# RWKV-7 mixer of a two-layer trunk: block inverse kept on VectorE, R and V projections moved among the first two chunks, VectorE and ScalarE in written order

## The chip, the cores and the metric

One NeuronCore of a Trainium2 chip. Its engines each run their own instruction stream: TensorE (PE, matmuls; PEld, its weight loads), VectorE (DVE), ScalarE (ACT), GpSimd (POOL) and SyncE (SP, which here only issues DMAs; ACT and POOL issue some too). The metric is the device time of one execution in microseconds; the times given are medians of three runs.

## The reference

The reference is a decoder trunk of two layers on 256 tokens of 1024 features. Each layer is LN(alpha x + SwiGLU/2), LN(alpha x + mixer), LN(alpha x + SwiGLU/2). The mixer of layer 0 is a spatial gating MLP, that of layer 1 is RWKV-7, which is where the change lies:

```python
r, k, v = jnp.einsum('nbsd,nde->nbse', x_rkv, w_rkv)      # six token-shift mixes of x
w = -jax.nn.softplus(-(w0 + jnp.tanh(xw @ w1) @ w2)) - 0.5
a = jax.nn.sigmoid(a0 + (xa @ a1) @ a2)
g = jax.nn.sigmoid(xg @ g1) @ g2
kk = normalise(k * k_k);  k = k * (1 + (a - 1) * k_a)
decay = jnp.exp(-jnp.exp(w))
# per head (16 heads x 64), token by token:
state = state * decay + (state @ -kk) (kk * a)^T + v k^T;   y = state @ r
y = group_norm(y) ; bonus = sum(r * k * r_k) * v
out = ((y + bonus) * g) @ w_o
```

## The kernel before

The recurrence is computed in four chunks of 64 tokens (two to each token tile `m` of 128). Within a chunk the token-by-token dependence is a unit-triangular system of 64x64 per head. Its matrix, the products of ZR (columns of -kk and r, decayed) with KBT (k and kk a, divided by the decay), is masked (`ab`) and cut into blocks of 32x32; the inverse of the 128 diagonal blocks is found on VectorE by 31 steps of two operations (`i0` to `i30`, L1034 and L1036), with one block in each partition; `H` holds the inverses. Getting from the masked matrix (tokens in partitions) to that layout (block in partition) goes through DRAM: `ab` writes to `dA` (GpSimd's queue), `iload` reads `M` (ScalarE's queue); afterwards `iout` writes `dH` and `dG` and reads `G` and `Hf` (SyncE's queue). `od0`, `od1`, `oe0`, `oe1` then compute the off-diagonal blocks on PE from `G`, `Hf` and the masked matrix. Each chunk `c` then runs `av` and `x` (right-hand side X), `u` (X times the inverse `Hf`, into VU), `s` (the state for the next chunk) and `y` (the output); `on` normalises the output per head on VectorE with a power operation on GpSimd in the middle (`rs`), `ga` makes the gate, `og` multiplies, `oc` transposes for the output projection `O`.

Projections run in units of 128 input rows x 1024 weights, one DMA of 512 KB each. K and the output projection multiply hi/lo pairs (three matmuls, L221 to L223); for them a weight unit is rounded by ScalarE (`wh`, L118) and its rest taken by VectorE (`wl`, L119). R and V run in plain float32 (L301) from the loaded unit itself.

Two things set the order. PE and SyncE run in program order, which the hand-written string ORDER gives: each word is an operation, `R011` is R, half 0, token tile 1, part 1. ACT, VectorE and GpSimd are ordered by a scheduler from dependencies. Weight loads and roundings are put in by `Stream.advance` some units ahead of their use (`ahead`). PSUM banks are two `tp`, two `mm` and four `acc`.

```python
        DX, DW, DA, DI, DO = A, nc.sync, G, A, nc.sync     # queues of decay_x, decay_w, ab, iload, iout
```

## Time and profile before

| | us |
|---|---|
| median of 3 runs (1144.19 to 1144.59) | 1144.59 |
| the profiled execution's own time | 1143.73 |
| its span, first to last instruction | 1142.0 |
| PE busy | 1103.9 |
| VectorE busy | 698.7 |
| ScalarE busy | 480.5 |
| GpSimd busy | 42.2 |

The RWKV mixer's own instructions lie between about 727 and 947 us of the span. Busy time of PE counts a matmul from its start to its modelled end, and the granted clock says in which of its two speeds PE ran (1.00 is 2.4 GHz, 0.50 is 1.2 GHz).

### The profile page before, as it was taken

What the parts mean: (1) busy time and instruction counts of PE and PEld (TensorE: products, weight loads), DVE (VectorE), ACT (ScalarE), POOL (GpSimd) and SP (SyncE); (2) the same over time, 40 slices, a digit from 0 to 9 for tenths busy, and PEclk for the clock granted to TensorE, in tenths of its full rate; (3) what the DMA queues carried; (4) which work ended last, traced back from release to release, by engine and by line L of the source; (5) the groups of instructions that cost most, each with busy time, mean ns of one, the idle gap of its engine ahead of it and who ended that gap; (6) DMA issues with size and microseconds to landing.
All of it is one profiled execution on the core that took longest, in us unless ns stands there. A gap on an engine that the chain in (4) does not pass through costs nothing.

```text
span 1142.0 us, 15347 instructions
## 1 busy us (share of the span) xinstructions
PE 1103.9 (97%) x5860; PEld 879.1 (77%) x5860; DVE 698.7 (61%) x969; ACT 480.5 (42%) x636; POOL 42.2 (4%) x44
## 2 busy tenths in 40 slices
PE   8999999999999999999999999999989889999997
PEld 5888888778888788888888888775555668788885
DVE  6654556769658555457655453878655787555544
ACT  5544443455335444444444452462123245444430
POOL 0000000100000000000000000112100110000000
PEclk9999999999999999999999999999999989999999
DMA  8776565775645766655677563437876146766530
GB/s 289 236 235 185 185 197 168 232 268 196 208 148 155 240 206 198 186 183 157 197 221 225 183 202 124 166 93 256 271 203 237 43 129 191 239 204 196 184 111 38
DMA packets 153933, 216.51 MB, mean 190 GB/s; under 512 B 21213, under 2 KB 114845, under 8 KB 153858
## 3 DMA queue, kind: packets, MB, share of 16 engines
...
q0 software_dynamic: 1024, 3.15, 1.0%
...
HBM read 209.46 MB, written 3.42 MB: 186 GB/s over the span
## 4 chain that ended last, share of the span: by engine, by line
PE 81%; DVE 7%; DMA 5%; issue 2%; ACT 2%; POOL 1%; ACTq 0%; SPq 0%; DVEq 0%; POOLq 0%
PE mm L221 15%; PE mm L223 15%; PE mm L222 15%; PE acc L221 8%; PE acc L222 8%; PE acc L223 8%; PE mm L301 3%; DMA raw<-ffn_w_in 2%; DVE wl L119 2%; PE tp L415 2%; POOL rs L259 1%; PE tp L235 1%; ACT wh L118 1%; DMA raw<-rwkv_w_rkv 1%; PE tp L577 1%
## 5 line engine op out<-in xcount | busy, mean ns | idle before, releaser
L119 DVE TENSOR_TENSOR wl<-raw,wh 128x1024 fp32r<-128x1024 f32 (+1 forms) x332 | 396.2, 1209 | 267.1 <-ACT wh L118 259.8
L118 ACT CAST wh<-raw 128x1024 fp32r<-128x1024 f32 (+1 forms) x332 | 340.3, 1041 | 340.8 <-PE acc L223 146.0
L221 PE MATMUL mm<-wh,xh 128*128 128x512 f32 x832 | 327.3, 393 | 5.5 <-ACT wh L118 2.4
L222 PE MATMUL mm<-wl,xh 128*128 128x512 f32 x832 | 324.7, 390 | 0.6 <-DVE wl L119 0.6
L223 PE MATMUL mm<-wh,xl 128*128 128x512 f32 x832 | 325.1, 391 | 0.2 <-DVE xl L228 0.2
L221 PEld LDWEIGHTS mm<-wh,xh 128*128 128x128 f32 x832 | 156.5, 188 | 41.5 <-ACT wh L118 3.9
L223 PEld LDWEIGHTS mm<-wh,xl 128*128 128x128 f32 x832 | 156.6, 188 | 34.6 <-DVE xl L228 1.9
L222 PEld LDWEIGHTS mm<-wl,xh 128*128 128x128 f32 x832 | 156.7, 188 | 33.1 <-DVE wl L119 1.3
L221 PE MATMUL acc<-wh,hT 128*128 128x512 f32 x352 | 141.4, 402 | 0.0
L222 PE MATMUL acc<-wl,hT 128*128 128x512 f32 x352 | 137.4, 390 | 0.0
L223 PE MATMUL acc<-wh,hT 128*128 128x512 f32 x352 | 137.4, 390 | 0.0
L404 ACT ACTIVATE h<-mm 128x256 f32<-128x256 f32 x88 | 33.8, 384 | 106.0 <-PE mm L223 105.9
L223 PEld LDWEIGHTS acc<-wh,hT 128*128 128x128 f32 x352 | 66.1, 188 | 14.8
L222 PEld LDWEIGHTS acc<-wl,hT 128*128 128x128 f32 x352 | 66.2, 188 | 12.6
L221 PEld LDWEIGHTS acc<-wh,hT 128*128 128x128 f32 x352 | 66.1, 188 | 12.7
L405 DVE TENSOR_TENSOR h<-h,mm 128x256 f32<-128x256 f32 x88 | 36.8, 418 | 59.8 <-ACT h L404 59.8
L301 PE MATMUL mm<-raw,mix 128*128 128x512 f32 x128 | 59.4, 609 | 0.9 <-DMA raw<-rwkv_w_rkv 0.9
L259 POOL TENSOR_TENSOR rs<-ve,mhalf 128x1 f32<-128x1 f32 x14 | 14.2, 1011 | 926.2 <-DVE ve L267 926.2
L301 PEld LDWEIGHTS mm<-raw,mix 128*128 128x128 f32 x128 | 23.6, 193 | 26.6 <-issue 23.8
L228 DVE TENSOR_TENSOR hT<-tp,hT 128x512 fp32r<-128x512 f32 x44 | 30.2, 686 | 7.6 <-ACT hT L227 7.6
L227 ACT CAST hT<-tp 128x512 fp32r<-128x512 f32 x44 | 25.9, 588 | 9.0 <-PE tp L415 8.9
L227 ACT CAST xh<-tp 128x512 fp32r<-128x512 f32 x24 | 13.2, 588 | 34.9 <-PE tp L235 34.9
...
## 6 DMA issues: line engine op xcount, KB each, us to landing
...
```

Source lines behind the costliest of these rows:

```text
L118: i = nc.scalar.copy(h[:, s], raw[:, s])
L119: j = nc.vector.tensor_tensor(l[:, s], raw[:, s], h[:, s].bitcast(F32), op=ALU.subtract)
L221: i = mm(out, lhsT=lh, rhs=rh, start=start, stop=False)
L222: mm(out, lhsT=lh, rhs=rl, start=False, stop=False)
L223: mm(out, lhsT=ll, rhs=rh, start=False, stop=stop)
L227: i = self.nc.scalar.copy(h, src)
L228: return i, self.nc.vector.tensor_tensor(l, src, h.bitcast(F32), op=ALU.subtract)
L259: self.nc.gpsimd.tensor_tensor(rs, v, self.mhalf[:, :w], op=ALU.pow)
L301: i = self.nc.tensor.matmul(ps, lhsT=xs[:, c], rhs=h[:, s], start=kk == 0, stop=kk == 7)
L404: nc.scalar.activation(hb[:, o + 256:o + 512], ps[:, 0:256], AF.Silu)
L405: nc.vector.tensor_tensor(hb[:, o:o + 256], hb[:, o + 256:o + 512], ps[:, 256:512], op=ALU.mult)
L415: nc.tensor.transpose(ps[:, o:o + P], st["h"][c][:, hh:hh + P], self.ident)
```

## The change

From `iload` to `free` VectorE and ScalarE keep the order in which the program is written, by dependencies that need no semaphore (class `Ordered`; its wrapper is at L149, so the changed kernel's instructions of the mixer carry that line); weight roundings are included. `ab` writes two tensors, `Aof` (off-diagonal blocks) and `D` (diagonal blocks, part of which ScalarE copies into place), and `M`, `G` and `Hd` are made by VectorE's 32x32 transposes; all DRAM copies of the inverse are gone. `Hf` is cleared by GpSimd instead of VectorE, and filled by two VectorE and two GpSimd copies for each token tile (`hf0`, `hf1`). R's PSUM is copied out by ScalarE (`rk`), its two products follow as `rm` and `rb`. `on` is cut in two, `on` up to the root and `oz` for the multiply with it. The `Ex` DMAs of `decay_x` go from ScalarE's queue to SyncE's. `od`, `oe` and `u`, `s` of the first two chunks use `acc` banks. R and V parts are single units, and those not done before the inverse is out are placed among the chunks; `x` comes ahead of `av`. `a:N` in ORDER sets how far roundings run ahead.

```diff
-                i = nc.scalar.copy(h[:, s], raw[:, s])
-                j = nc.vector.tensor_tensor(l[:, s], raw[:, s], h[:, s].bitcast(F32), op=ALU.subtract)
+                i = self.A.copy(h[:, s], raw[:, s])
+                j = self.V.tensor_tensor(l[:, s], raw[:, s], h[:, s].bitcast(F32), op=ALU.subtract)
...
+class Ordered:
+    def __init__(self, b, eng):
+        self.b, self.eng, self.on, self.last = b, eng, False, None
+    def __getattr__(self, name):
+        fn = getattr(self.eng, name)
+        def f(*args, **kw):
+            i = fn(*args, **kw)
+            if self.on:
+                if self.last is not None:
+                    self.b.after(i, self.last)
+                self.last = i
+            return i
+        return f
...
+        V, A = self.ws.V, self.ws.A = Ordered(self, nc.vector), Ordered(self, nc.scalar)
...
-                R, bo = st["R"][m]
-                rk = self.s4("rk")[:, 0:512]
-                s = slice(h * 512, h * 512 + 512)
-                V.tensor_tensor(R[:, s], ps, st["E"][m][0][:, s], op=ALU.mult)
-                V.tensor_tensor(rk, ps, st["kp"][m][:, s], op=ALU.mult)
+                    st["rk", m] = self.s4("rk")
+                s = half(h)
+                A.copy(st["rk", m][:, s], ps)
+            return f
+        def rmul(m, h):
+            def f():
+                R, s = st["R"][m][0], half(h)
+                (V.tensor_tensor(R[:, s], st["rk", m][:, s], R[:, s], op=ALU.mult))
+            return f
+        def rbonus(m, h):
+            def f():
+                s = half(h)
+                rk, bo = st["rk", m][:, s], st["R"][m][1]
+                (V.tensor_tensor(rk, rk, st["kp"][m][:, s], op=ALU.mult))
...
+                if c == 0 and m == 0:
+                    st["D"], st["Aof"] = self.s4("D"), self.s4("Aof")
+                b0 = (m * 16 + c * 8) * 32
+                D, Of = (st[k][:, b0:b0 + 256] for k in ("D", "Aof"))
...
-                masked(t[:, half(c)], ps, self.mask[:, 0:64])
-                if c == 0:
-                    return
-                t3 = t.rearrange("p (b z) -> p b z", z=64)
-                for blk in range(2):
-                    for e in range(2):
-                        b0 = blk * 64 + e * 32 + m * 16
-                        r0 = e * 64 + blk * 32
-                        DA.dma_start(self.dA[b0:b0 + 16].rearrange("b s t -> s b t"),
-                                    t3[r0:r0 + 32, :, blk * 32:blk * 32 + 32])
+                p3 = ps.rearrange("p (b t) -> p b t", b=8)
+                for out, k in ((Of, 32), (D, 0)):
+                    V.tensor_tensor(out.rearrange("p (b t) -> p b t", b=8), p3[:, :, k:k + 32],
+                                    self.mask[:, k:k + 32].unsqueeze(1).broadcast_to([P, 8, 32]), op=ALU.mult)
+                for e in range(2):
+                    r = slice(e * 64 + 32, e * 64 + 64)
+                    A.copy(D[r, :], Of[r, :])
...
-            DI.dma_start(st["M"], self.dA.rearrange("b s t -> b (s t)"))
+            V.on = A.on = True
+            V.transpose(st["M"].rearrange("p (s t) -> p t s", s=32), st["D"].rearrange("p (b t) -> p t b", b=32))
...
-                V.memset(t, 0.0)
+                G.memset(t, 0.0)
...
-            Mt, Ht = st["M"], st["H"]
-            M3, H3 = (t.rearrange("p (s t) -> p s t", s=32) for t in (Mt, Ht))
-            q = DO
-            q.dma_start(self.dH.rearrange("b s t -> b (s t)"), Ht)
-            V.tensor_copy(M3[0:64], H3[0:64].rearrange("p s t -> p t s"))
-            Hf = st["Hf"]
-            q.dma_start(self.dG.rearrange("b s t -> b (s t)"), Mt[0:64, :])
-            Gt = self.s4("G")
-            st["G"] = Gt
-            def back(m, blk, e):
-                b0 = blk * 64 + e * 32 + m * 16
-                r0 = e * 64 + blk * 32
-                q.dma_start(
-                    Hf[m].rearrange("p (b t) -> p b t", t=64)[r0:r0 + 32, :, blk * 32:blk * 32 + 32],
-                    self.dH[b0:b0 + 16].rearrange("b s t -> s b t"))
-            for e in range(2):
-                q.dma_start(Gt.rearrange("p (b t) -> p b t", t=32)[e * 64:e * 64 + 32],
-                            self.dG[e * 32:e * 32 + 32].rearrange("b s t -> s b t"))
-            for m in range(2):
-                for blk in range(2):
+            H = st["H"]
+            t = self.s4("G")
+            (V.transpose(t.rearrange("p (b s) -> p s b", b=32), H.rearrange("p (s t) -> p s t", s=32)))
+            st["G"] = t
+            st["Hd"] = self.s4("Hd")
+            V.transpose(st["Hd"].rearrange("p (b t) -> p t b", b=32), H.rearrange("p (s t) -> p t s", s=32))
+        def inv_fill(m):
+            def f():
+                for blk in (1, 0):
                     for e in range(2):
-                        back(m, 1 - blk, e)
+                        r = slice(e * 64 + blk * 32, e * 64 + blk * 32 + 32)
+                        out = st["Hf"][m].rearrange("p (b t) -> p b t", t=64)[r, :, blk * 32:blk * 32 + 32]
+                        src = st["Hd"][r, m * 512:m * 512 + 512].rearrange("p (b t) -> p b t", t=32)
+                        (V.tensor_copy if e else G.tensor_copy)(out, src)
...
+                    (A.copy if e else V.tensor_copy)(
+                        st["Hf"][m].rearrange("p (b t) -> p b t", t=64)[d0:d0 + 32, :, 32:64],
+                        ps[d0:d0 + 32, :].rearrange("p (b t) -> p b t", t=32))
...
+                ps = self.accb() if c_.ch < 2 else self.tpb()
...
-                rs = self.rsqrt(s2, 8)
-                V.tensor_tensor(yn, yn, per_head(rs, 8), op=ALU.mult)
+                st["rs", m, e] = self.rsqrt(s2, 8)
+            return f
+        def outz(m, e):
+            def f():
+                yn = st["yc", m].rearrange("p (b e j) -> p b e j", b=8, e=2)[:, :, e, :]
+                V.tensor_tensor(yn, yn, per_head(st["rs", m, e], 8), op=ALU.mult)
...
-        DX, DW, DA, DI, DO = A, nc.sync, G, A, nc.sync
+        DX, DW = nc.sync, nc.sync
...
+                elif t[:2] == "a:":
+                    self.ahead = int(t[2:])
...
-ab00 R000 mixG01 cZ10 R001 cZ11 cB11 ab01 cR00 mixR10 V100 ab10 ab11 iload i0 g1_0 mixG10 R100 i1 i2 i3 R101 dw1
-mixV10 p:gn_b kn01 i4 cR01 i5 st0 mixG11 mixV11 V010 cK00 sc000 V011 i6 i7 i8 rs0 i9 kb1 g2 cK10 cK11 i10 i11 V101
-g1_1 cK01 i12 i13 i14 sc001 V110 i15 sc010 i16 kb0 V111 i17 mixR11 i18 i19 i20 i21 i22 i23 i24 i25 st1 vu00 sc011
-i26 i27 ga00 i28 i29 av0 vu01 x0 i30 iout R010 od0 od1 oe0 bo00 oe1 bo01 u0 gb R011 s0 R110 cR10 av1 vu10 x1 R111
...
+ab00 R000 R001 mixG01 cZ10 R002 R003 cZ11 cB11 ab01 mixR10 rm00 mixR11 ab10 ab11 iload i0 i1 cR00 R100 R101 i2 i3 cK00 i4 i5 i6
+cK10 V100 V101 i7 i8 kn01 i9 cK01 V102 V103 i10 i11 R102 R103 dw1 i12 i13 i14 hz R010 R011 i15 i16 rm01 cR01 i17 i18 i19 i20 sc000 R012 R013 i21 i22 i23
+cK11 i24 i25 rs0 kb0 vu00 kb1 R110 R111 i26 sc001 i27 i28 x0 av0 i29 R112 i30 iout g1 od0 hf0 od1 oe0 oe1 u0 sc010 s0 hf1 sc011 g1_0 vu01 mixV10 R113
```

ScalarE, at the decay of token tile 0 (`Ep`, `Em` its exponentials, `Ex` the shifted one, `mh` a rounded mix, `th` and `ah` the low-rank inputs). Before:

```order
L811 ACTIVATE Ep_5936<-acc 128x512
L812 ACTIVATE Em_5937<-acc 128x512
L811 ACTIVATE Ep_5936<-acc 128x512
L812 ACTIVATE Em_5937<-acc 128x512
L821 DMA Ex_5938<-Ep_5936 63x1024
L822 DMA Ex_5938<-c_one 1x1024
L821 DMA Ex_5938<-Ep_5936 63x1024
L822 DMA Ex_5938<-c_one 1x1024
L227 CAST mh_5954<-mix_5953 128x512
L789 ACTIVATE th_5981<-tp 64x128
L790 COPY ah_5982<-tp 64x128
```

In the changed kernel (L149 is the wrapper's line, the names are the same):

```order
L149 ACTIVATE Ep_5933<-acc 128x512
L149 ACTIVATE Em_5934<-acc 128x512
L149 ACTIVATE Ep_5933<-acc 128x512
L149 ACTIVATE Em_5934<-acc 128x512
L149 CAST mh_5947<-mix_5946 128x512 x2
L149 ACTIVATE th_5972<-tp 64x128
L149 COPY ah_5973<-tp 64x128
```

The four `Ex` issues are no longer ahead of `mh`, `th` and `ah`; they stand on SyncE.

VectorE, from the last masks of `ab` (`Aab`) to the first steps of the inverse. Before, with mixes and R's products (`Ep`, `rk`, `bonus`) between them:

```order
L974 TENSOR_TENSOR Aab_6392<-tp,mask 128x512
L761 SCALAR_TENSOR_TENSOR mix_6490<-xx_5912,muT,xf_5911 128x128
L761 SCALAR_TENSOR_TENSOR mix_6378<-xx_5912,muT,xf_5911 128x128 x4
L906 TENSOR_TENSOR Ep_5936<-mm,Ep_5936 128x512
L907 TENSOR_TENSOR rk_6479<-mm,kp_5908 128x512
L908 TENSOR_TENSOR rk_6479<-rk_6479,r_k_6281 128x512
L909 TENSOR_REDUCE bonus_6327<-rk_6479 128x8
L1034 TENSOR_TENSOR T_6435<-H_6271,M_6433 128x31
L1036 TENSOR_TENSOR H_6271<-H_6271,T_6435 128x31
```

In the changed kernel:

```order
L149 SCALAR_TENSOR_TENSOR mix_6359<-xx_5909,muT,xf_5908 128x128 x3
L149 TENSOR_TENSOR Aof_6271<-tp,mask 128x256
L149 TENSOR_TENSOR D_6270<-tp,mask 128x256
L149 TENSOR_TENSOR Aof_6271<-tp,mask 128x256
L149 TENSOR_TENSOR D_6270<-tp,mask 128x256
L149 STREAM_TRANSPOSE M_6411<-D_6270 128x32x32
L149 TENSOR_TENSOR T_6413<-H_6260,M_6411 128x31
L149 TENSOR_TENSOR H_6260<-H_6260,T_6413 128x31
```

The transpose and the first step follow the last mask; R's products left this place.

VectorE at the end of the mixer, in the normalisation of the last two chunks (`sa`, `sb` sums per head, `yc` the centred output, `rs` from GpSimd, `wl` weight roundings of the output projection and the next stage). Before:

```order
L1221 TENSOR_TENSOR yc_7492<-acc,sa 128x8x64 x2
L119 TENSOR_TENSOR wl_7562<-raw_7066,wh_7561 128x1024
L1224 TENSOR_REDUCE sb<-o_7493 128x8 x2
L1225 TENSOR_SCALAR sb<-sb 128x8
L228 TENSOR_TENSOR xl_7470<-tp,xh_7469 128x512
L1227 TENSOR_TENSOR yc_7492<-yc_7492,rs 128x8x64
L1225 TENSOR_SCALAR sb<-sb 128x8
L119 TENSOR_TENSOR wl_7569<-raw_7072,wh_7568 128x1024
L1227 TENSOR_TENSOR yc_7492<-yc_7492,rs 128x8x64
L119 TENSOR_TENSOR wl_7576<-raw_7551,wh_7575 128x1024
L1234 TENSOR_TENSOR yc_7492<-yc_7492,gn_g_5962 128x512 x2
```

In the changed kernel:

```order
L149 TENSOR_TENSOR wl_7499<-raw_7323,wh_7498 128x1024
L149 TENSOR_REDUCE sa<-acc 128x8
L149 TENSOR_SCALAR sa<-sa 128x8
L149 TENSOR_TENSOR yc_7486<-acc,sa 128x8x64
L149 TENSOR_REDUCE sb<-o_7487 128x8
L149 TENSOR_SCALAR sb<-sb 128x8
L149 TENSOR_TENSOR wl_7522<-raw_7351,wh_7521 128x1024
L149 TENSOR_TENSOR yc_7486<-yc_7486,rs 128x8x64
L149 TENSOR_TENSOR wl_7542<-raw_7426,wh_7541 128x1024
L149 TENSOR_TENSOR yc_7486<-yc_7486,rs 128x8x64
L149 TENSOR_TENSOR wl_7556<-raw_7446,wh_7555 128x1024
L149 TENSOR_TENSOR yc_7486<-yc_7486,gn_g_7195 128x512
```

The two halves go one after the other, and a rounding stands in a fixed place between each sum and its multiply.

## Rows read from the trace of the kernel before

**Rows 1.** The page, its head and part 1.
```profile
span 1142.0 us, 15347 instructions
...
PE 1103.9 (97%) x5860; PEld 879.1 (77%) x5860; DVE 698.7 (61%) x969; ACT 480.5 (42%) x636; POOL 42.2 (4%) x44
```

**Rows 2.** Windows by stage: window, length, busy us of PE, PEld, DVE, ACT, POOL, clock, DMA.
```profile
727.00:792.00 65.00, 61.40 (x286) 40.89 (x286) 51.14 (x109) 31.98 (x55) 9.32 (x6) 0.97 0.52 175
792.00:850.00 58.00, 52.22 (x330) 29.54 (x330) 41.67 (x109) 10.42 (x25) 8.35 (x14) 1.00 0.80 253
850.00:914.30 64.30, 56.95 (x1003) 42.55 (x1003) 38.07 (x60) 18.63 (x26) 3.61 (x2) 0.92 0.43 140
914.30:947.20 32.90, 28.17 (x123) 22.36 (x121) 28.21 (x43) 13.37 (x17) 5.05 (x3) 0.90 0.47 145
```

**Rows 3.** Windows of 4 or 8 us, the same columns.
```profile
748.00:752.00 4.00, 4.00 (x10) 2.39 (x9) 3.12 (x10) 3.48 (x6) 0.00 (x0) 0.65 0.05 14
852.00:860.00 8.00, 6.81 (x186) 6.31 (x181) 2.73 (x4) 1.69 (x4) 0.00 (x0) 0.50 0.83 270
932.00:936.00 4.00, 4.00 (x14) 3.16 (x13) 3.85 (x6) 1.17 (x2) 0.00 (x0) 0.50 0.44 128
820.00:824.00 4.00, 3.07 (x13) 1.66 (x12) 3.69 (x10) 1.69 (x5) 0.00 (x0) 1.00 1.04 395
```

**Rows 4.** PE's timeline: start, duration, line, operation, wait before it and releaser.
```profile
747.62 1.12 PE L799 MATMUL acc<-a,ah 65*128 65x512 f32 x2 [1.49 <-ACT ah L790]
...
777.05 0.63 PE L235 MATMUL tp<-ident,a 128*128 128x128 f32 x4 [1.21 <-DVE a L875]
...
820.23 1.04 PE L235 MATMUL tp<-ident,Em 128*128 128x128 f32 x8
...
825.74 2.34 PE L1186 MATMUL tp<-g,mix 128*128 128x160 f32 x16
...
834.79 1.16 PE L1013 MATMUL tp<-ZR,KBT 64*128 64x128 f32 x16
...
835.88 3.70 PE L301 MATMUL mm<-raw,mix 128*128 128x512 f32 x8
...
849.57 0.22 PE L1079 MATMUL tp<-G,Aab 32*32 32x32 f32 x2 [1.23 <-DMA G<-dG]
...
931.40 1.94 PE L235 MATMUL tp<-ident,o 128*128 128x128 f32 x8 [3.82 <-DVE o L1236]
```

**Rows 5.** ScalarE's timeline (ACTq: its DMA issues).
```profile
743.44 1.33 ACTq L821 DMA_DIRECT2D Ex<-Ep  x1
...
746.51 0.62 ACT L227 CAST mh<-mix 128x512 fp32r<-128x512 f32 x1 [2.61 <-DMA Ex<-Ep]
```

**Rows 6.** VectorE's groups, 727 to 960: count, busy us, mean ns, idle time before.
```profile
L119 DVE TENSOR_TENSOR wl<-raw,wh 128x1024 fp32r<-128x1024 f32 x22 | 26.4, 1216 | 1.4 <-ACT wh L118 1.4
...
L974 DVE TENSOR_TENSOR A<-tp,mask 128x512 f32<-128x512 f32 x16 | 10.3, 686 | 4.1 <-PE tp L1013 3.9
...
L1227 DVE TENSOR_TENSOR yc<-yc,rs 128x512 f32<-128x512 f32 x4 | 2.8, 693 | 4.8 <-POOL rs L259 4.8
...
L1042 DVE MEMSET Hf<- 128x1024 f32 x2 | 1.8, 912 | 0.3 <-issue 0.3
```

**Rows 7.** VectorE's timeline around the inverse.
```profile
799.60 0.68 DVE L974 TENSOR_TENSOR Aab<-tp,mask 128x512 f32<-128x512 f32 x1
...
812.05 0.18 DVE L1034 TENSOR_TENSOR T<-H,M 128x31 f32<-128x31 f32 x1
...
838.59 0.22 DVE L1036 TENSOR_TENSOR H<-H,T 128x31 f32<-128x31 f32 x1
...
838.84 1.05 DVE L1049 COPY M<-H 64x1024 f32<-64x1024 f32 x1
```

**Rows 8.** GpSimd's groups, whole span.
```profile
L512 POOL TENSOR_SCALAR_AFFINE_SELECT wsp<-wsp 128x1024 f32<-128x1024 f32 x2 | 2.6, 1298 | 0.8 <-DMA wsp<-sgu_w_sp 0.5 <-PE tp L235 0.2
...
L259 POOL TENSOR_TENSOR rs<-sb,mhalf 128x8 f32<-128x8 f32 x4 | 7.7, 1930 | 89.0 <-DVE sb L1225 89.0
```

More of the change, by code (lines that the diff above doesn't have):

```diff
@@ L66, in __init__ @@
         self.behind = ()
+        self.V, self.A = tc.nc.vector, tc.nc.scalar
         self.ring = [None] * (N_W + N_WX)
@@ L1124, in vu, with x @@
                 return st["VU"][c_.ch][rows, h * 64:h * 64 + 64]
+            def x(c_):
+                c_.X = self.small("X", [P, 512])
+                if c_.ch:
+                    ps, S0 = self.mmb(), st["S", c_.ch]
+                    for h in range(NH):
+                        mm(ps[par(h), col(h)], lhsT=c_.zr(h, 0), rhs=S0[par(h), col(h)], start=True, stop=True,
+                           tile_position=((h % 2) * 64, (h % 2) * 64))
+                    A.copy(c_.X, ps)
             def av(c_):
@@ L1130, in av @@
                        tile_position=(c_.c * 64, (h % 2) * 64))
-                X = c_.X = self.small("X", [P, 512])
-                A.copy(X, ps)
-            def x(c_):
                 if c_.ch:
-                    ps, S0 = self.mmb(), st["S", c_.ch]
-                    for h in range(NH):
-                        mm(ps[par(h), col(h)], lhsT=c_.zr(h, 0), rhs=S0[par(h), col(h)], start=True, stop=True,
-                           tile_position=((h % 2) * 64, (h % 2) * 64))
                     V.tensor_tensor(c_.X, c_.X, ps, op=ALU.add)
+                else:
+                    A.copy(c_.X, ps)
             def rs(c_):
```

72 lines of the change are left out of this document (33 added, 39 removed).

## The prediction

> **What bounds the kernel now.** The head of the page comes first: TensorE (PE) is busy for 1103.9 us of a span of 1142.0 [rows 1]. The change leaves PE's matmuls as they are and only reorders them, and only inside the RWKV mixer, from 727 to 947 us. So the time is matmuls plus PE's waits plus what a halved clock costs, and I keep that ledger by stage. In the windows cut at the places where the change bites, span minus busy gives PE's idle time [rows 2]: A (727 to 792, projections and decay) 65.0 - 61.4 = 3.6; B (792 to 850, scores, inverse, R and V units) 58.0 - 52.2 = 5.8; C (850 to 914.3, four chunks) 64.3 - 56.95 = 7.35; D (914.3 to 947.2, normalisation, output projection) 32.9 - 28.2 = 4.7. Together 21.5. The second cost shows only in the column of the granted clock. After some of the waits it stands at 0.50 or 0.65, where 0.50 is 1.2 of 2.4 GHz [rows 3]: 748 to 752 loses 4 x 0.35 = 1.4; 852 to 860 loses half of 6.8 busy, 3.4; 932 to 936 loses 2.0. That is 6.8 more, so no reordering can gain over 21.5 + 6.8 = 28.3 us.
>
> What ends the waits is read from PE's timeline [rows 4]: 1.49 for `ah` from ScalarE, 1.21 for `a` from VectorE, 1.23 for `G` from a DMA, 3.82 for `o` from VectorE. The rest are waits of under 1.7 at hand-overs.
>
> **A: 4.1 gained.** The matmul at 747.62 waits 1.49 for `ah`. On ScalarE, `mh` and behind it `ah` stand behind four `Ex` DMA issues from 743.44 on; `mh` waited 2.61 there [rows 5]. The change issues these DMAs from SyncE. 2.61 is more than 1.49, so this wait goes, and with it the slow clock right behind it, 1.4. The wait of 1.21 for `a` goes too: two memsets of 0.91 each [rows 6] leave VectorE ahead of that operation, and 1.8 is more than 1.21. On SyncE the issues stand ahead of weight loads; I cost this under the DMA term. A = -1.49 - 1.21 - 1.4 = -4.1.
>
> **B: 4.4 gained.** Today the inverse's first operation starts at 812.05, 12 us after the last mask (799.60), because the masked blocks go out to DRAM and back; its last starts at 838.59, and `G` is on the chip at 849.57, 11 us later, by two more trips [rows 4, 7]. The new chain on VectorE starts from the last of the `ab` masks. These come earlier, since two V units (`V100`) no longer stand ahead of them on PE: a pair of units takes 3.5 from start to start, so 1.75 each (3.70 with its drain [rows 4]). PE then ends `ab11` at 795.2, its masks at about 796.5. From there, in the written order:
> - transpose of `D` 1.1, the 62 operations 23.3 (26.8 from 812.05 to 838.8, less the three mask pairs of the scores that lie between them, six masks of 0.6 net, 3.5 [rows 6, 7]);
> - `kn01` 0.6, `rm01` 0.6 and about 1 of wait for R's last unit;
> - two mask pairs of the scores 2.4 and about 2.5 of wait, because `sc001` stands behind `R110` and `R111` on PE;
> - transpose to `G` 1.1.
> The sum is 32.6, so `G` is ready at 829.1. PE has between `ab11` and `od0` 15 units (26.25), six transposes of four (0.5 each, 3.0), and `sc000`, `sc001`, `av0` (1.1 each, 3.3): 795.2 + 32.55 = 827.8, with 0.9 of wait before `cK01` 828.7. The two sides meet, and PE waits 0.9 + 0.5 = 1.4 in this stage where it waited 5.8. The work that left (three units 5.25, two `g1` of 2.4 with their small waits, `ga00` 2.1, `sc010` and `sc011` 2.2, about 16 with what hung on it) isn't saved; it now stands among the chunks. B = 1.4 - 5.8 = -4.4.
>
> Two prices in that chain have no row. A 32x32 stream transpose of 128x1024: nearest row below is a copy of 64x1024, 1.055 [rows 7]; above I take four times that, 4.2. I take 1.1, because that copy already reads H transposed in its free dimension. At 4.2, `G` is 6.2 later and B is +1.8. The Trainium skill, "Vector Engine (DVE) Microarchitecture Reference", section 3.8, says that the 32x32 transpose is pipelined at one element per cycle and lane; with the 0.96 GHz of its page "VectorE: DVE Perf Modes" 1024 columns would be an estimated 1.07, and the sum would stay as it is; no run here shows the operation.
>
> The other price is a GpSimd copy of 32x512 (four fill `Hf`). The nearest row is GpSimd's select over 128x1024, 1.30, halved 0.65; the far one its tiny power operation, 1.93 [rows 8]. `u0` needs `Hf` only after `od0`, `od1`, `oe0`, `oe1`, about 5.4 us of PE after `G`. Behind `G` come `Hd` 1.1 and, side by side, two VectorE and two GpSimd copies: 1.1 + 2 x 0.65 = 2.4, or 1.1 + 3.9 = 5.0 at the far price, covered either way. The Trainium skill ("SBUF — State Buffer", section "SBUF: two separate sides") speaks against this split: a VectorE copy in a two-port mode and a GpSimd operation lock each other out of a shared port. Then the copies would run one after the other: 1.1 + 2 x 0.6 + 2 x 0.65 = 3.6, or 6.2 with the far price, 0.8 late: the sum by it is unchanged or 0.8 worse.
>
> **C: 1.1 gained.** Before: 7.35 idle + 3.4 slow clock = 10.75. After, I list PE's waits by the new order: `s0` 0.4 for VectorE's copy of VU, `g1_0` 1.4 for a bank, `gs` twice 0.8, `sc111` 2.8 (its masks stand behind `on00`, `on01`, `oz00`, `rb10`, `rb11`, `bo00` on VectorE, with two banks only), `x3` 1.7 for the state: with small ones 7.9. The offdiagonal products are the same small matmuls that ran at half clock; with units between them I keep half of the loss, 1.7. C = 9.6 - 10.75 = -1.1.
>
> **D: 1.5 lost.** The 3.82 before the output's transposes is the chain on VectorE from the last `y` to the last `o`: four reductions, subtractions and squares, then waits for GpSimd's root (4.8 for four, about 1.2 each), then four multiplies [rows 6]. Splitting the normalisation lets VectorE round weights (1.22 each [rows 6]) during the root. But the scheduler already put such roundings there, so about 17 us of VectorE work lie between `y3` and the last `o` in both. What is new: the order is fixed, so the second `xl` half stands behind `ln0` (0.5 at `O41`), and the next stage's first `xl` behind six roundings (1.4 less 0.4 of cover, 1.0). The slow clock at 932 stays.
>
> **DMA: 1.0 lost.** From 792 to 850 the kernel moves 253 GB/s, with a peak of 395 [rows 2, 3]. Fifteen units of 512 KB (7.9 MB) and 1.5 MB of `KB` in some 37 us are 254 on the mean, about the same, but runs of six units back to back need 0.52 MB / 1.75 = 300. And the `Ex` issues, up to 1.33 each [rows 5], now hold the loads behind them on SyncE for some 3 us a set, twice. Loads already under way hide a part; I take 1.0, between nothing and 4, which 9.4 MB cost at a tenth less than 254 (41 in place of 37). The DRAM trips that leave are small, and what they hid behind needs no other cover.
>
> **Sum.** -4.1 - 4.4 - 1.1 + 1.5 + 1.0 = -7.1. The profiled execution took 1143.73, 1.73 over its span, so 1136.6; the median of the runs shown is 0.86 higher, so **1137.5**.
>
> **Rivals.** What a measurement here can tell from no change is about 0.2%, 2.3 us: 1142.3 to 1146.9.
> - *Better (0.16).* C's slow clock goes (-1.7), its waits halve because VectorE no longer runs low-priority work ahead of the chunks' (-3.9), D and DMA cost nothing (-2.5): 1129.4. For it: the waits of C are hand-overs of 0.4 to 1.7. Against it: the chain x, u, s, y is serial.
> - *No change (0.10).* The written order makes VectorE hand on each wait that the free scheduler filled with roundings; PE merely meets them behind `od0`. B's gain of 4.4 and C's 1.1 are given back: 1143.
> - *Slower (0.14).* In the changed program 49 of the 101 VectorE instructions from `u0`'s copy to the last `o` wait for another engine (counted in its written order), and each now holds all behind it. At 0.28 us extra per hand-over that is 13.7 us on the chain; less the 7.1, about 1144 + 6 = 1150. It decides from 7.1 / 49 = 0.15 each. For it: VectorE is 28.2 of 32.9 busy in D [rows 2], so no slack there. Against it: in C VectorE is 38 of 64 busy.
> - The change may fail to do what it says: the chain would be paced by PE at `rm01` and `sc001` and the removed trips worth only the wait that they end today, 1.2 of the 4.4; the sum is then 3.2 less good, 1140.7. That lies inside the main case.
>
> **How the numbers follow.** The sum's own case has 0.60, with its range 1130 to 1142: one transpose at twice the price (+1.1), the DMA term from 0 to 4, the clock in C from 0 to 3.4. Faster is that case and the better one, 0.76; same 0.10; slower 0.14. The range that leaves out no more than 2 in 10 cuts off the best tail (all of C's waits gone) and the worst of the slower case: 1127 to 1147.
>
> **What would show it.** PE has no wait at `acc<-a,ah` behind `Ex`, and the clock there is 1.00. The stream transpose takes 1.1. `G` is ready within 1 us of PE's arrival at `od0`, some 33 us after the last mask. PE's idle in C is 8, its longest wait at `sc111`; the output's transposes wait 4 as before. The prediction is wrong if the transposes take 3 us or more, if the clock halves through the chunks, or if weight units wait for their loads by more than 4 us.

## The result, and the profile after

| | before | changed |
|---|---|---|
| median, us (15 runs each) | 1144.59 (1141.92 to 1148.68) | 1153.41 (1147.99 to 1166.81) |
| ratio, 95% interval | | 1.0083 [1.0061, 1.0105] |
| profiled execution, us | 1143.73 | 1149.83 |
| its span, us, and mean granted clock | 1142.0, 0.988 | 1148.1, 0.984 |

The kernel is slower by 0.8%, outside the range that was given and 3.4 over the time of the rival on the other side (1150). Its executions also spread more, and the spread goes with the clock: one of 1148.04 has a mean granted clock of 0.988, one of 1161.83 has 0.974.

The head of the page answers to [rows 1]:

```profile
PE 1108.7 (97%) x5860; PEld 881.4 (77%) x5860; DVE 705.7 (61%) x975; ACT 486.5 (42%) x650; POOL 42.2 (4%) x42
```

As before, PE is busy 97% of the span; that number alone tells nothing of the loss. What tells it is the ledger of the prediction, taken in both traces between the same marks on PE: from the second token tile's transposes of x at the mixer's start (736.81 before, 733.46 after) to the same transposes at the start of the next stage (955.76 and 962.13). Idle is the window less PE's busy time; slow clock is busy time times one minus the granted clock, summed over windows of 1 us (so it is the time that these matmuls would have saved at 1.00); the rest is PE's work at full clock. A ends at the first `ab`, B at `od0`, "C and D" at the next stage's first transposes.

| us, before -> changed | length | idle | slow clock | work |
|---|---|---|---|---|
| A | 44.7 -> 40.0 | 2.7 -> 0.0 | 1.7 -> 0.0 | 40.3 -> 39.9 |
| B | 68.0 -> 55.9 | 6.1 -> 7.1 | 0.0 -> 1.7 | 62.0 -> 47.1 |
| C and D | 96.3 -> 117.4 | 12.1 -> 13.7 | 7.3 -> 11.2 | 77.0 -> 92.5 |
| next stage's start | 9.9 -> 15.5 | 0.2 -> 2.9 | 0.0 -> 3.1 | 9.6 -> 9.4 |
| sum | 219.0 -> 228.7 | 21.1 -> 23.8 | 9.0 -> 16.0 | 188.9 -> 188.9 |

PE's work is the same to 0.1 us. So in these two executions the loss between the marks, 9.7, is 2.7 of waits and 7.0 of slow clock. How the loss divides is not fixed: in a second profile of the changed kernel (below) the length is 225.9, with 25.2 of idle time and 11.3 of slow clock, so there the loss is 6.9, of which 4.1 are waits and 2.3 slow clock. (The profiled spans differ by 6.1 only, because the code ahead of the mixer, which is the same, ran 3.4 shorter in this execution.) Windows of the changed kernel by stage, with the columns of [rows 2]; the last is the next stage's start:

```profile
733.46:773.42 39.96, 39.93 (x171) 26.93 (x170) 31.90 (x68) 26.58 (x45) 7.24 (x5) 1.00 0.39 123
773.42:829.29 55.87, 48.79 (x305) 25.79 (x304) 40.49 (x102) 13.13 (x30) 6.04 (x9) 0.97 0.73 225
829.29:914.25 84.96, 75.07 (x1033) 53.29 (x1033) 51.60 (x89) 21.76 (x37) 6.42 (x6) 0.86 0.33 109
914.25:950.00 35.75, 29.63 (x177) 22.84 (x176) 31.26 (x45) 14.17 (x18) 5.83 (x3) 1.00 0.60 203
950.00:959.00 9.00, 8.36 (x23) 6.30 (x24) 9.00 (x15) 5.70 (x6) 0.93 (x1) 0.62 0.63 200
```

The four stretches in which the clock fell, columns of [rows 3]:

```profile
800.00:804.00 4.00, 4.00 (x7) 1.60 (x6) 3.69 (x10) 0.51 (x2) 1.70 (x4) 0.57 0.80 218
832.00:840.00 8.00, 7.45 (x176) 7.13 (x176) 2.43 (x4) 3.67 (x7) 2.01 (x4) 0.50 0.16 43
886.00:900.00 14.00, 13.56 (x118) 9.04 (x118) 4.95 (x8) 1.16 (x2) 0.00 (x0) 0.52 0.28 87
951.00:957.00 6.00, 5.62 (x13) 4.46 (x14) 6.00 (x11) 4.30 (x5) 0.15 (x1) 0.50 0.47 149
```

And PE's timeline at the long waits, as in [rows 4]:

```profile
799.20 0.63 PE L255 MATMUL tp<-ident,Em 128*128 128x128 f32 x4 [2.55 <-DVE Em L149]
...
829.29 2.30 PE L1104 MATMUL acc<-G,Aof 32*32 32x32 f32 x128 [1.41 <-DVE G L149]
...
886.44 2.67 PE L1044 MATMUL tp<-ZR,KBT 64*128 64x128 f32 x16 [4.11 <-DVE A L149]
...
903.80 1.15 PE L1157 MATMUL mm<-S,ZR 64*64 64x64 f32 x32 [1.52 <-DVE S L149]
...
950.00 0.50 PE L241 MATMUL mm<-wh,xh 128*128 128x512 f32 x1 [2.28 <-ACT xh L149]
```

The wait of 2.55 at 799.20 stands ahead of the stretch at 800, that of 4.11 at 886.44 ahead of the one at 886, that of 2.28 at 950.00 ahead of the one at 951. `od0` at 829.29 still waits for `G`, now 1.41 and for VectorE, and the stretch from 831 on begins in the 32x32 matmuls, as in the kernel before. The two waits that [rows 4] showed in A are gone, and the 3.82 at `o` is 0.62.

What PE waits for is read on the engine named. VectorE around the inverse (compare [rows 7]):

```profile
788.38 0.41 DVE L149 TENSOR_TENSOR D<-tp,mask 128x256 f32<-128x256 f32 x1
790.46 2.11 DVE L149 STREAM_TRANSPOSE M<-D 128x1024 f32<-128x1024 f32 x1 [1.67 <-ACT D L149]
...
827.33 1.91 DVE L149 STREAM_TRANSPOSE G<-H 128x1024 f32<-128x1024 f32 x1
829.10 2.01 DVE L149 STREAM_TRANSPOSE Hd<-H 128x1024 f32<-128x1024 f32 x1
```

A stream transpose of 128x1024 takes 1.9 to 2.1, not 1.1, and the first one also waits 1.67 for ScalarE, which copies half of `D` into place. From the last mask's end (788.8) to `G` (829.2) it is 40.4 us. VectorE ahead of `sc111`:

```profile
881.15 0.68 DVE L149 TENSOR_TENSOR rk<-rk,kp 128x512 f32<-128x512 f32 x1
...
883.20 0.68 DVE L149 TENSOR_TENSOR vb<-vb,bonus 128x512 f32<-128x512 f32 x1
885.09 0.69 DVE L149 TENSOR_TENSOR vb<-vb,gn_b 128x512 f32<-128x512 f32 x1 [1.21 <-DMA gn_b<-rwkv_gn_b]
885.70 1.28 DVE L149 TENSOR_TENSOR A<-tp,mask 128x512 f32<-128x512 f32 x2
```

The masks of `sc110` (`A`, 885.70), which free the two banks that `sc111` needs, stand behind the bonus products (`rk`, `bonus`, `vb`) and a wait of 1.21 for `gn_b`, though PE had done `sc110` at 882.3. ScalarE at the next stage's start:

```profile
946.21 1.06 ACT L149 CAST wh<-raw 128x1024 fp32r<-128x1024 f32 x1 [3.27 <-DMA raw<-ffn_w_in]
948.42 1.04 ACT L149 CAST wh<-raw 128x1024 fp32r<-128x1024 f32 x1 [1.16 <-DMA raw<-ffn_w_in]
949.37 1.07 ACT L149 CAST xh<-tp 128x512 fp32r<-128x512 f32 x2
```

The next stage's `xh` (949.37) is written behind two casts of weights that wait for their DMA, 3.27 and 1.16.

### The profile page after: what moved, and what is told of

It reads as the page before. It is cut to its first block, busy times and chain, and to the rows that moved or that the text cites. A ratio compares the mean times of both kernels' runs of the same rounds, so it can differ in the third digit from the quotient of the medians.

```text
span 1148.1 us, 15342 instructions
## 1 busy us (share of the span) xinstructions
PE 1108.7 (97%) x5860; PEld 881.4 (77%) x5860; DVE 705.7 (61%) x975; ACT 486.5 (42%) x650; POOL 42.2 (4%) x42
## 3 DMA queue, kind: packets, MB, share of 16 engines
HBM read 208.15 MB, written 2.11 MB: 183 GB/s over the span
## 4 chain that ended last, share of the span: by engine, by line
PE 83%; DVE 7%; DMA 5%; ACT 2%; issue 1%; POOL 1%; SPq 0%; DVEq 0%; ACTq 0%; POOLq 0%
PE mm L241 16%; PE mm L243 16%; PE mm L242 15%; PE acc L241 8%; PE acc L243 8%; PE acc L242 8%; DMA raw<-ffn_w_in 3%; PE mm L321 3%; DVE wl L149 2%; PE tp L435 2%; PE tp L255 1%; ACT wh L149 1%; PE tp L1044 1%; PE tp L806 1%; PE tp L597 1%
## 5 line engine op out<-in xcount | busy, mean ns | idle before, releaser
L149 DVE TENSOR_TENSOR wl<-raw,wh 128x1024 fp32r<-128x1024 f32 (+1 forms) x332 | 396.3, 1209 | 266.7 <-ACT wh L149 258.8
L149 ACT CAST wh<-raw 128x1024 fp32r<-128x1024 f32 (+1 forms) x332 | 340.2, 1041 | 336.5 <-PE acc L243 141.7
L149 DVE TENSOR_TENSOR hT<-tp,hT 128x512 fp32r<-128x512 f32 x44 | 30.1, 685 | 7.6 <-ACT hT L149 7.6
L149 ACT CAST hT<-tp 128x512 fp32r<-128x512 f32 x44 | 25.9, 588 | 9.0 <-PE tp L435 8.9
L301 DVE SCALAR_TENSOR_TENSOR y<-acc,x 128x512 f32<-128x512 f32 x24 | 15.9, 686 | 18.8 <-PE acc L243 18.8
```

Source lines behind the costliest of these rows:

```text
L149: i = fn(*args, **kw)
L301: nc.vector.scalar_tensor_tensor(y[:, s], acc[n], c, x[:, s], op0=ALU.mult, op1=ALU.add)
```

## The experiments

The ratio of each is to the kernel before, measured beside it, with its 95% interval; the median stands behind it. Runs that were measured beside the same runs of the kernel before are called a series. Four theories to begin with. Two are on the clock. **C**: a long wait of PE is paid twice, as a wait and as slow clock behind it. **S**: the clock falls because the chunks are small matmuls, whatever PE waits for. Two are on the order. **W** puts the loss down to the written order on VectorE and ScalarE, **P** to PE's new order.

### The written order taken away

```diff
-            V.on = A.on = True
```

> The changed kernel without the written order on VectorE and ScalarE: the scheduler orders these two again, all else (transposes on VectorE, ORDER, banks, DMAs) stays. Theory W (the written order is the loss: each hand-over holds what stands behind it): the wait before sc111 (4.1 us) and that at the first matmul of the next stage (2.3 us) shrink to under 1.5 each, with the slow clock behind them, and the time comes to 1138 to 1144, at or below the kernel before. Theory P (PE's new order is the loss: chunks without enough other work between them): the waits stay, the clock still halves after them, and the time stays at 1147 to 1156.

Measured: 1.0004 [0.9985, 1.0023], 1146.66. W is right that the loss goes: without the written order the kernel is no slower than before. It is not right on the gain: the time doesn't go under that of before (1138 to 1144 was expected). The waits named in the expectation shrink, that before `sc111` to 2.1 and that of the next stage to 0.2, but the output's transposes now wait 5.0 for `o`. The profiled execution took 1152.44, the longest of the twelve, so its ledger is read with care (idle 20.7, slow clock 19.8), and a second one was taken:

> The changed kernel without the written order once more, for a second profile, since the first profile was the slowest of its twelve runs. If slow clock is what differs between executions, the work between the two marks is again 188 us and idle time again 20 to 21, and the slow clock is nearer to 12 than to 19.8. The ratio to before stays at 0.998 to 1.002.

Measured: 1.0014 [0.9994, 1.0034], 1147.15; between the marks work 187.7, idle 21.7, slow clock 20.1. The ratio came as expected; that the slow clock would be nearer to 12 did not. Both profiles lose 11.5 to the clock in one and the same stretch, from 898 to 922, and took 1152.44 and 1153.13, where the medians are 1146.66 and 1147.15. Why, stays open.

### The order ended ahead of the last two chunks

```diff
-... mixG11 a:0 V110 on00 g1_1 ...
+... mixG11 a:0 V110 free on00 g1_1 ...
-... O71 free
+... O71
```

> The changed kernel with the written order on VectorE and ScalarE ended ahead of on00, so that it holds from iload through the first two chunks only. Theory W2 (the written order costs where normalisation, bonus and weight roundings share VectorE with the last two chunks): the time is that of the kernel without any written order, ratio to before 0.998 to 1.002. Rival (it costs in the inverse and the first chunks): the ratio stays at 1.006 to 1.010.

Measured: 1.0031 [1.0012, 1.0050], 1149.62, between the two expectations; the changed kernel itself, run again in the same series:

> The changed kernel once more, for a second profile beside the first and on the chip of the three others. If the slow clock follows PE's waits, it falls at the same four places as in the first profile (800, 831, 886 and 950 us), and profiles differ in how long it lasts at each; the sum of PE's work is the same 188.8 us between the two marks. If the clock halves at random, the places differ.

Measured: 1.0053 [1.0035, 1.0071], 1152.04. The clock fell at 801, 835, 890 and 952, at the same four waits (2.6, 1.4, 3.8, 2.7), and lost 1.5, 4.9, 3.3 and 1.5 where the first profile had 1.7, 4.7, 6.6 and 3.1; PE's work between the marks is 189.4, near the 188.8 expected. So in these two profiles the places are the same, and how long the clock stays down is not. Ending the order ahead of `on00` brings back 0.2%, with intervals that overlap (and that overlap with those of the kernel without any written order), so it doesn't tell where the written order costs.

### The wait before sc111 filled with work

```diff
-... bo00 sc110 bo01 vu10 sc111 av2 ...
+... bo00 sc110 fill bo01 vu10 sc111 av2 ...
+        def fill():
+            ps = self.mmb()
+            for n in range(36):
+                mm(ps[:, :P], lhsT=self.ident, rhs=self.ident, start=True, stop=True)
```

> The changed kernel with 36 extra 128x128x128 matmuls of the identity on PE, about 4 us, put between sc110 and sc111, where PE waits 4.1 us; their result is not used. The masks that sc111 waits for do not depend on them. Theory C (the halved clock follows the wait): sc111 starts when it did, PE's idle time falls by about 4, the clock behind it stays at 1.00, and the time falls by the clock's share alone, 6 us: 1142 to 1147. Rival S (the clock halves because of the small matmuls of the chunks): the clock still halves, the time is that of the changed kernel or up to 1 us more.

Measured: 1.0045 [1.0029, 1.0060], 1151.71, in neither expectation. The matmuls took 8.3 us, twice what was planned, so that they held PE some 4.4 past the wait. Still C and D lost 4.7 to the slow clock instead of 11.2. With 16 of them:

> As the run with 36 dummy matmuls in the wait before sc111, with 16 of them: these took 0.245 us each there, so 16 are 3.9 us, under the wait of 4.1, and PE should start sc111 at the same moment as without them. Theory C (the slow clock follows PE's wait): C and D lose 6.5 us less to the slow clock, the waits elsewhere stay, and the median is 5 to 7 under that of the changed kernel. Rival S (the clock halves because of the chunks' small matmuls, or of its own accord): the time of the changed kernel within 2 us.

Measured: 1.0014 [1.0003, 1.0025], 1149.26, which is 0.4% under the changed kernel in the same series (2.8 us by the medians, 4.5 by the ratios; 5 to 7 was expected). PE's timeline, in which each of the 16 is two records, and the window behind it:

```profile
887.00 3.84 PE L1362 MATMUL mm<-ident 128*128 128x128 f32 x32
891.26 1.75 PE L1044 MATMUL tp<-ZR,KBT 64*128 64x128 f32 x16 [0.42 <-DVE A L149]
```

```profile
893.00:903.00 10.00, 8.40 (x137) 5.09 (x136) 5.90 (x10) 2.79 (x4) 0.00 (x0) 1.00 0.17 65
```

`sc111` still waits for the same masks (0.42 behind the filler, 4.3 in all), and the ten microseconds behind it, the same small matmuls, run at a granted clock of 1.00 where the changed kernel had 0.52 (and, in its second profile, half clock from 890 to 897). That shows C at this place: with the wait filled, the clock stays up, and these matmuls by themselves don't bring it down.

### The wait before sc111 taken away by order

```diff
-... V112 rb10 oz01 rb11 g2 V113
-p:gn_g bo00 sc110 bo01 vu10 sc111 av2 rs2 ...
+... V112 oz01 g2 V113
+sc110 vu10 sc111 av2 rs2 rb10 rb11 p:gn_g bo00 bo01 ...
```

> The changed kernel with four groups of VectorE work (rb10, rb11, bo00, bo01, some 6.7 us) moved in the written order from ahead of the masks of sc110 and sc111 to behind rs2. Theory C (a long wait of PE costs twice, once as a wait and once as the halved clock behind it): the wait of 4.1 before sc111 falls to about 1, the granted clock between that place and the next 14 us is 1.00 instead of 0.5, and the time falls by 3 + 6.5 = 9.5 from the profiled 1149.8 to about 1140 to 1144. Rival S (the clock halves because the chunks are small matmuls): only the wait goes, 3 us, about 1147.

Measured: 1.0034 [1.0020, 1.0048], 1150.49. The wait fell to 0.8, and the clock held from there (888) to 903; but the 6.7 us of VectorE work now stood ahead of the state: the wait for `S` before `x3` grew from 1.5 to 2.5 with a slow clock of 3.4 behind it, and the gate waited 1.3 for a parameter's DMA. Idle between the marks stayed at 23.8. Half of what was gained at `sc111` was given back at the next hand-over, and the time is over both expectations.

### The roundings at the end, and three waits at once

```diff
-... og10 a:3 O40 og11 a:2 O50 a:1 O60 a:0 O70 oc10 O01 O11 oc11 ln0 a:1 a:2 O21 a:3 O31 a:4 O41 ...
+... og10 O40 og11 O50 O60 O70 oc10 O01 O11 oc11 ln0 O21 O31 O41 ...
```

> The changed kernel without the numbers that hold the weight roundings back at the end (from O30 on they run four units ahead again, in the written order). Theory T (the wait of 2.3 + 0.6 at the next stage's first matmuls is ScalarE's casts in front of it, which wait for weights that were loaded late because the roundings were held back): that wait and the 3.1 us of slow clock behind it go, and the time falls by 4 to 6. Rival: the extra roundings in front of the output's last operations delay these, the wait moves to the output's transposes, and the time stays within 2 us of the changed kernel.

Measured: 1.0096 [1.0065, 1.0128], 1154.76. The mechanism of T was right and the rival won: the next stage's first matmul waits 0.24, but the roundings now stand ahead of the output projection's `xl`:

```profile
936.95 0.80 PE L243 MATMUL acc<-wh,xl 128*128 128x512 f32 x1 [2.86 <-DVE xl L149]
...
952.12 0.50 PE L241 MATMUL mm<-wh,xh 128*128 128x512 f32 x1 [0.24 <-ACT xh L149]
```

with 3.1 of slow clock from 936.3 on, where the changed kernel had none. This profile also shows a limit of C. PE waits 2.50 for `Em` up to 801.77, as in the changed kernel, whose program is the same up to there, but the clock stays at 1.00:

```profile
800.00:801.00 1.00, 0.00 (x0) 0.00 (x0) 0.93 (x4) 0.00 (x0) 0.00 (x0) 1.00 0.93 274
802.00:803.00 1.00, 1.00 (x6) 0.62 (x5) 0.93 (x3) 0.57 (x2) 0.82 (x2) 1.00 0.75 289
```

So a wait of this length can have slow clock behind it and need not. Then all three at once (in the next diff only what is new):

```diff
-... i7 i8 kn01 i9 cK01 ...
+... ab10 ab11 kn01 iload ... i7 i8 i9 cK01 ...
-... u2 og00 ga01 s2 a:1 og01 x3 ...
+... u2 rb11 bo01 ga01 s2 og00 a:1 x3 og01 ...
```

> The changed kernel with three long waits of PE taken away by order alone, the written order kept: kn01 ahead of iload (2.6 us at cK01), rb and bo behind sc111 and og00 behind s2 (4.1 before sc111, 1.5 before x3), roundings four ahead at the end (2.9). Theory C (each wait of over 1.5 us costs itself and the slow clock behind it): idle time falls by some 9 and slow clock by some 10, 1153 - 15 to 19 = 1134 to 1138 at the median, clearly under the kernel before. Rival S (the waits move to the next hand-over and the small matmuls are slow anyway): 1146 to 1152.

Measured: 1.0030 [1.0011, 1.0049], 1149.66. The list of PE's waits (total, times, longest):

```profile
PE acc L243 <- DVE xl L149: 2.8, 1, 2.8
PE mm L321 <- DMA raw<-rwkv_w_rkv: 2.8, 3, 1.4
PE tp L1235 <- DMA g<-rwkv_g: 2.2, 1, 2.2
PE mm L1157 <- DVE S L149: 2.2, 1, 2.2
PE acc L1104 <- DVE G L149: 1.4, 1, 1.4
```

The waits of 2.6 and 4.1 are gone, and idle is still 23.6: loads, a parameter, the state and `xl` took their place. Slow clock fell to 10.7. The time is the rival's (1146 to 1152), not C's (1134 to 1138). With PE work put into the waits for `G` and `Q` as well:

```diff
-... R112 i30 iout g1 od0 hf0 od1 oe0 oe1 u0 sc010 s0 ... mixV10 R113
+... R112 i30 iout R113 g1 od0 hf0 od1 sc010 oe0 oe1 u0 s0 ... mixV10
```

> As the kernel with three waits taken away, and one more: the unit R113 ahead of od0 and the scores sc010 between od1 and oe0, so that PE has work while it waits for G (1.4) and for Q (1.0). Theory C: the slow clock of 4.7 us that follows there in the changed kernel (from 831 to 842) goes or shrinks to under 2, and the time is 4 to 6 under that of the three. Rival (the 32x32 matmuls of od and oe bring the slow clock by themselves): 1 to 2 us less idle, the clock stays at 0.50 there, and the time is 1 to 2 under that of the three.

Measured: 1.0063 [1.0040, 1.0086], 1152.29. The wait for `G` went, and `od`, with `sc010` behind it, ran at 1.00. One wait of 1.7 came in `oe`, at 838.5, and the clock fell behind it, at 840.6 (4.3 lost):

```profile
833.00:834.00 1.00, 1.00 (x74) 1.00 (x70) 0.90 (x2) 0.64 (x2) 0.10 (x1) 1.00 0.74 191
841.00:842.00 1.00, 0.47 (x2) 0.29 (x2) 0.49 (x1) 0.48 (x1) 0.00 (x0) 0.50 0.00 0
```

Both expectations had a gain over the run before it, and there was none; nor did `od` and `oe` bring the slow clock by themselves here, as S had it.

### The parts of the change by themselves

Stage A in the kernel before:

```diff
-        DX, DW, DA, DI, DO = A, nc.sync, G, A, nc.sync
+        DX, DW, DA, DI, DO = nc.sync, nc.sync, G, A, nc.sync
-                V.memset(t, 0.0)
+                G.memset(t, 0.0)
-... p:k_a dec01 dc0 mixK10 ... lw10 mixK11 K010 ...
+... p:k_a dec01 mixK10 ... lw10 mixK11 dc0 K010 ...
```

> The kernel before with stage A of the change alone: the Ex DMAs on SyncE, issued after mixK11 as in the change, and the two memsets of Hf on GpSimd. Inverse, DRAM trips and order are those of before. If the 3.6 us that stage A gained (no wait for ah or a, no slow clock behind it) come from these two moves, stage A has under 0.5 us of idle and the time is 0.2 to 0.4% under the kernel before. If they come from the rest of the new order, stage A is as before and so is the time.

Measured: 0.9963 [0.9949, 0.9976], 1141.62, as expected; stage A has 0.8 of idle (under 0.5 was expected) and no slow clock. Once more, beside the run that follows:

> Stage A of the change alone once more, beside the run that adds the inverse, on the same chip: ratio to before 0.995 to 0.998, so that the two differ by the inverse and by nothing else.

Measured: 0.9971 [0.9958, 0.9983], 1142.20. To it, the inverse of the change alone (its `ab`, `iload`, `iout`, `hf`, `od` and `oe`, scheduled freely, in the order of before):

```diff
-... iout R010 od0 od1 oe0 ...
+... iout R010 od0 hf0 od1 hf1 oe0 ...
```

> The kernel before with stage A of the change and with the inverse alone of the change: VectorE's transposes, the split masks, Hf filled by VectorE and GpSimd; order, R's products, banks and scheduling as before. If the new inverse is good in itself (no wait for G, 1.2 to 1.8 us; od0 comes no earlier since the same 16 units stand ahead of it): 1 to 2 us under stage A alone, ratio to before 0.994 to 0.996. If three transposes of 2 us and the copies lengthen VectorE's chain by as much as the trips cost: the ratio of stage A alone, 0.996, or up to 1.000.

Measured: 1.0047 [1.0029, 1.0065], 1151.17: 0.8% slower than stage A alone on the same chip, outside both expectations. The wait for `G` is gone, but two others came on PE, ahead of `od0` by 60 and 40 us:

```profile
791.23 1.09 PE L235 MATMUL tp<-ident,Ep 128*128 128x128 f32 x4 [2.87 <-DVE D L995]
...
811.27 1.07 PE L235 MATMUL tp<-ident,Ep 128*128 128x128 f32 x4 [2.38 <-DVE Ep L906]
```

The first is for `D`: a mask holds the PSUM bank that PE's next transposes need (by the names in the trace, `tp` is all that the two share), and on VectorE

```profile
787.34 1.39 DVE L761 SCALAR_TENSOR_TENSOR mix<-xx,muT,xf 128x128 f32<-128x128 f32 x5
789.13 0.69 DVE L908 TENSOR_TENSOR rk<-rk,r_k 128x512 f32<-128x512 f32 x1 [0.39 <-DMA r_k<-rwkv_r_k]
789.74 0.42 DVE L995 TENSOR_TENSOR Aof<-tp,mask 128x256 f32<-128x256 f32 x1
790.07 0.68 DVE L909 TENSOR_REDUCE bonus<-rk 128x8 f32<-128x512 f32 x1
790.66 0.42 DVE L995 TENSOR_TENSOR D<-tp,mask 128x256 f32<-128x256 f32 x1
```

the mask that frees it (790.66) comes behind mixes and R's products, by the scheduler's choice. Where one mask of 512 columns freed the bank, now two of 256 must pass. The second is not for a bank but for data: the transposes read `Ep`, R's product, which VectorE begins at 810.53, 1.6 after PE has ended R's unit:

```profile
801.86 7.03 PE L301 MATMUL mm<-raw,mix 128*128 128x512 f32 x16
...
810.53 0.68 DVE L906 TENSOR_TENSOR Ep<-mm,Ep 128x512 f32<-128x512 f32 x1
```

From 802.6 to 810.6 VectorE runs the first steps of the inverse, and the product stands behind them. In stage A alone these steps still wait for the DRAM trip; VectorE has been idle for 9.1 when R's unit ends, and takes the product at once (804.57), so that PE waits 0.8. B lost 4.8 to the slow clock, some 3.2 of it behind these two waits, where stage A alone lost none; the rest, from 845.5 on, has only a wait of 0.8 ahead of it. In the same trace the clock also falls where PE had hardly waited, inside the 32x32 matmuls of `od` and `oe` (from 851.3 on):

```profile
853.00:854.00 1.00, 0.69 (x44) 0.58 (x39) 0.00 (x0) 0.96 (x3) 0.00 (x0) 1.00 0.66 123
854.00:855.00 1.00, 1.00 (x64) 0.91 (x58) 0.00 (x0) 0.94 (x2) 0.00 (x0) 1.00 0.90 334
855.00:856.00 1.00, 1.00 (x58) 0.99 (x57) 0.68 (x1) 0.17 (x1) 0.00 (x0) 0.87 0.97 156
856.00:857.00 1.00, 0.89 (x26) 0.79 (x22) 0.50 (x1) 0.41 (x1) 0.00 (x0) 0.50 0.88 254
```

PE is idle for 0.3 in the five microseconds ahead of the fall at 855.7. There S holds, and in two more profiles the clock falls in `oe` behind as little idle time: at 832.6 in the first one without the written order, and at 859.2 in the run that follows. In 16 of the 17 profiles here the clock falls in the stretch of `od`, `oe` and `u`, and such a fall loses 2.3 to 5.6; but in the others PE has also been idle for 1.4 or more in the four microseconds before, and in the one exception, with the wait for `G` filled, `od` and `oe` ran at 1.00. So this stretch speaks for S in three traces and is not settled. And the whole change in the order of before:

```diff
-            V.on = A.on = True
-R000 R001 ... ab10 ab11 iload i0 i1 cR00 ...
+R000 R001 ... R002 R003 rm00 rb00 ... ab10 ab11 iload i0 g1_0 ... (every word of the old ORDER, its pairs of units written out)
```

> The inverse on VectorE without DRAM trips, the Ex DMAs on SyncE, the split normalisation and the banks of the change, but the order of the kernel before (its ORDER, with the two new pieces rm and rb right behind R's units and the fill right behind od0 and od1), and no written order on VectorE and ScalarE. If the removal of the trips is worth what the trace of before shows: stage A gains 3.6, the wait of 1.2 for G goes, od0 comes no earlier as 16 units stand ahead of it, and the time is 1138 to 1141. If the transposes and copies on VectorE cost more than they free (three transposes of 2 us each): 1143 to 1147.

Measured: 1.0118 [1.0095, 1.0141], 1158.93, the slowest of all and over both expectations; idle 29.2, slow clock 15.5. It was measured in the same series as the changed kernel without the written order (1.0004), from which it differs by ORDER alone. So P is wrong: with the new inverse in place, PE's new order is worth 1.1%, and of the 12.3 us between the medians 5 stand in stage A, which takes 45.3 here and 40.0 there in the profiles.

Last, the kernel before with stage A and a filler at its longest wait:

```diff
-... O50 O60 O70 oc10 ...
+... O50 O60 O70 fill oc10 ...
```

> The kernel before with stage A of the change alone, and 14 dummy matmuls (some 3.4 us) on PE between the last output projection and the transposes of o, where PE waits 3.8 us for VectorE and the clock then halves (3.1 us lost in the profile). Nothing that VectorE does depends on them. Theory C: the wait turns into work of the same length, the clock stays at 1.00 behind it, and the time falls by 2 to 3 us against stage A alone (ratio to the kernel before 0.993 to 0.995). Rival S: the ratio stays at 0.996, or rises by the time that the dummies hold PE past the end of the wait.

Measured: 0.9951 [0.9934, 0.9967], 1141.60. In stage A alone the windows at the wait and behind it read:

```profile
926.00:930.00 4.00, 0.73 (x4) 0.27 (x2) 4.00 (x7) 0.00 (x0) 0.00 (x0) 0.99 0.59 193
930.00:937.00 7.00, 6.43 (x19) 5.22 (x20) 6.53 (x11) 2.22 (x3) 0.00 (x0) 0.52 0.30 94
```

With the filler, PE and the window behind it:

```profile
924.68 3.29 PE L1324 MATMUL mm<-ident 128*128 128x128 f32 x28
928.66 1.23 PE L235 MATMUL tp<-ident,o 128*128 128x128 f32 x8 [0.69 <-DVE o L1236]
```

```profile
930.00:936.00 6.00, 5.78 (x24) 4.50 (x25) 6.00 (x12) 3.68 (x4) 0.76 (x1) 1.00 0.30 87
```

The clock stays at 1.00, which is C again in another kernel. In time it is not told apart from stage A alone (0.9963 and 0.9971, intervals overlap); 0.993 to 0.995 was expected.

## Why the prediction was wrong

Between the marks -7.1 was forecast and +9.7 measured. Of these 16.8 the slow clock makes 10.1 (3.1 less was forecast, 7.0 more came) and PE's idle time 6.7.

- **A was right.** 4.1 was forecast; idle and slow clock fell by 4.4, and alone it is worth 0.3 to 0.4% in two series. Of the parts run by themselves it is the one that pays.
- **B, first step that failed: the price of the chain.** The transposes were taken at 1.1 each and are 1.9 to 2.1; the first waits 1.67 for ScalarE's copies of `D`, which the sum left out; `rm01` waits 2.95 for R's last unit, and the two mask pairs 1.93 and 3.10. So `G` comes 40.4 after the last mask and not 32.6. That it came at 829.2, where 829.1 was written, is chance: the chain began 7.7 earlier than written and was 7.8 longer. PE took 39.9 from `ab11` to `od0` where 33.5 was forecast (4.3 of it idle, 1.7 slow clock), so that they still meet (1.41): B's idle time was forecast to fall by 4.4 and rose by 1.0, with 1.7 of slow clock on top and 2.6 at `cK01` for `kn01` where 0.9 was forecast. The Trainium skill, "Vector Engine (DVE) Microarchitecture Reference", section 3.8, gives one element per cycle and lane, an estimated 1.07 for 1024 columns with the clock of its page "VectorE: DVE Perf Modes"; the trace doesn't agree, with 1.91 to 2.11.
- **B, the gain itself.** "G earlier" was costed as if VectorE's new work were free of consequences for PE. The run with the inverse alone shows that it costs 0.8% in the order of before: PE waits for a mask that frees a PSUM bank and for R's product, which now stands behind the inverse's steps. The trips through DRAM were slow but left VectorE free for such work, and PE had 16 units to do meanwhile.
- **C, the step that failed by most: "I keep half of the loss, 1.7".** Of slow clock the prediction granted 3.7 in all; 16.0 came, and 11.3 in the second profile. It costed waits one by one and gave each its own length only. The idle time of C itself was less far off (7.9 forecast, 9.9 measured). `sc111` was forecast at 2.8, measured 4.1, with 6.6 of slow clock behind it; filled with work, that clock loss fell to nothing in the ten microseconds behind it.
- **D and the next stage.** Forecast 1.5 worse. The wait for `o` went (3.8 to 0.6), which was not forecast, but PE waits 3.0 for `wh`, `wl`, `xh` and `xl` in its place, and the next stage's start lost 5.6 instead of the 1.0 given: its inputs stand behind casts that wait for late loads, since the roundings and so the loads had been held back.
- **DMA** was of the right size for R's and V's units: 0.7 of waits for loads in the first profile and 2.0 in the second, against 1.0 in a range of 0 to 4.
- **The rivals.** "Slower" gave 1150 at 0.14 and named the written order. The order's removal brings back 0.4 to 0.8% (1.0053 and 1.0083 against 1.0004 and 1.0014, in different series), so the mechanism was in part right; but the trace doesn't show 0.28 us at each of 49 hand-overs. Seven waits of over 1 us make 14.2 of its 23.8 of idle time, and four of them have slow clock at or behind them. The forecast's own sign of being wrong, "if the clock halves through the chunks", came in part: it halved from 831 to 842 and from 886 to 900, and stood at 1.00 between.

What stays open: without the written order the kernel gains back to the time of before and no further, and the ledger of its profiled executions doesn't stand for its median; when a wait of 1.5 us or more has slow clock behind it and when not; what the split normalisation, the moved copies and the banks are worth, which were not run alone; and why PE's idle time comes to 20 to 25 us in every variant that keeps the changed order of PE, however the waits are moved, was not taken apart further. The version that beats both kernels is stage A alone, 0.3 to 0.4% under the kernel before.
